# A hybrid attention and state-space step on one core: TensorE's order in the loop over head groups, fixed as written

## The chip, the cores and the metric

The kernel runs on one core of a Trainium2 chip. The metric is the device time of one execution in microseconds (us), median of several runs. Engines: TensorE (PE, with PEld for its weight loads), VectorE (DVE), ScalarE (ACT), GpSimd (POOL), and SyncE (SP), which issues the DMAs.

## The reference, cut to what matters

Two layers run over 128 context tokens and 512 latent tokens. Layer 0 is attention. Layer 1, where the change lies, is a Mamba-2 scan in both directions over chunks of 128 tokens:

```python
proj = h @ w_in
z, xbc, dt = split(proj)
xbc = silu(depthwise_conv_centred(xbc, conv_w, conv_b))       # -> xs, bs, cs
# per chunk, per direction
y_diag = einsum('bclsgr,bcsgrp->bclgrp', cb[..., None] * decay, x)
states = einsum('bclgn,bclgrp->bcgrpn', b, x * decay_end[..., None])
h_next = h * chunk_decay + states
y_off  = einsum('bclgn,bcgrpn->bclgrp', c, h_prev) * exp(a_cs)
# both directions and the skip term summed
y = rms_norm(y * silu(z), gnorm_w)
out = y @ w_out
```

There are 32 heads in 4 groups of 8. A group shares B and C.

## The kernel before, in words

Tokens lie in five tiles t of 128: tile 0 is the context, tiles 1 to 4 the latent tokens. `layer1` loops over the head groups g (0 to 3), and in each over ten steps j. A step emits, in this order: `off` (L1172: the state's part of the output), `advance` (L1179: the next state), `prompt_state` (L1150), `decay` (a small product C times B, L1116, and the chain that makes the decay matrix), `diag` (L1134: the diagonal products of one tile, then L1137: four transposes of Y), loads, and then the step's fill work: a projection of 128 columns (`proj_T`, L914, 48 products, "a unit" below) for the next group's x, B and C or for this group's z, and transposes of the unit before (`x_turn`, `b_turn`, L1007). In group 3 the fills of steps 3 to 8 are pieces of the output projection (`part_mm`, L1366, 24 products each), fed by `part_turn`, which loads gated rows back from DRAM into the two buffers named `u`.

One decay matrix passes through a chain: two DMAs into buffers `am0` and `am1` (`a_load`, L1112), two selects on POOL (L1120, L1121), sixteen exponentials on ACT (L1125), an add on POOL (L1126), a product on DVE (L1127), then `diag`. There are two `am0` buffers and one `am1`. So the load of `am0` for tile 1 (fourth in the order 0, 2, 3, 1, 4) waits for the diagonal products of tile 2, and that of `am1` for tile 4 waits for tile 1's add.

TensorE's small outputs go to a PSUM pool `a` of four buffers, and units to a pool `pj` of two. `gate` multiplies by z, squares and sums (L1086, L1078, L1090); `gate_last` does it in group 3, and `final_rstd` (L1371) takes the sum over partitions with a product on TensorE.

What is emitted is not the order on the engines: the kernel is built with a scheduler that plays the program against its own cost model and writes out an order for each engine and for SP's queue. Each engine then runs its own list strictly in that order.

Of the kernel before, what the change touches and what calls it, by code (L numbers as in the profile page):

```python
# [26 lines left out]
NG = 4  # L27
# [26 lines left out]
class Hybrid:  # L54
# [955 lines left out]
    def layer1(self, hT, wp, pj, pa, ctx):  # L1010
        nc, tc, A, O = self.nc, self.tc, self.A, self.O
# [19 lines left out]
        def x_turn(g, jj):  # L1031
            xt = xts[g]
            self.turn(wcur["u"], pa, lambda t, ps: nc.scalar.copy(xt[:, t, P * jj:P * jj + P], ps))

        def bc_unit(g, which):
            if which == 0:
                wcur["bc"] = self.load_w(wp, A["l1_w_in"], [(2 * DI + P * g, P), (2 * DI + P * (NG + g), P)])
                bcs[g] = {"T": self.tl(sp, [P, NT, P], tag="T")}
            wcur["u"] = bcs[g][which] = self.conv_chunk(16 + 4 * which + g, wcur["bc"], P * which, hT, pj, self.tl(sp, [P, TW - 3], tag=f"B{which}"))

        def b_turn(g):
            T = bcs[g]["T"]
            self.turn(bcs[g][0], pa, lambda t, ps: nc.scalar.copy(T[:, t, :], ps))
# [16 lines left out]
        def z_unit(g, jj):  # L1060
            zs, off_ = z_tile(g, jj)
            ps = self.proj_T(pj, wcur["z"], off_, P, hT)
            z_evac(zs, ps[:, 0:TW - 2])
# [41 lines left out]
        def y_init(g, t):  # L1105
            y = Y[:, t].rearrange("p j q -> p (j q)")
            nc.gpsimd.tensor_tensor(h3(y), h3(xts[g][:, t, :]), bch(self.dsk[:, 8 * g:8 * g + 8]), op=ALU.mult)

        def a_load(g, t):
            af = W[g, t] = [self.tl(wk, [P, 8, P], tag=f"am{d}", bufs=2 - d) for d in range(2)]  # L1110
            for d in range(2):
                nc.sync.dma_start(out=af[d].rearrange("p h l -> p (h l)"), in_=self.acd[t][g][d].rearrange("h l -> (h l)").unsqueeze(0).to_broadcast([P, 8 * P]))  # L1112
# [16 lines left out]
        def diag(g, t):  # L1129
            w = W.pop((g, t))[0]  # L1130
            pd = self.tl(pa, [P, 4, P], tag="a")
            for h in range(8):
                e = 64 * (h % 2)
                nc.tensor.matmul(pd[e:e + 64, h // 2, :], xts[g][:, t, HD * h:HD * h + HD], w[:, h, :], start=True, stop=True)  # L1134
            pr = self.tl(pa, [P, 4, P], tag="a")
            for i in range(4):
                nc.tensor.transpose(pr[:, i, :], Y[:, t, i, :], self.ident)  # L1137
            nc.scalar.copy(Y[:, t], pd)
            nc.vector.tensor_tensor(Y[:, t], Y[:, t], pr, op=ALU.add)
# [5 lines left out]
        def prompt_state(g, d):  # L1145
            xw = Xw.pop((g, 0, d))
            T = bcs[g]["T"]
            ps = self.tl(pa, [P, 4, P], tag="a")
            for j in range(4):
                nc.tensor.matmul(ps[:, j, :], xw[:, P * j:P * j + P], T[:, 0, :], start=True, stop=True)  # L1150
            st = self.tl(wk, [P, 4, P], tag="ym")
            nc.scalar.copy(st, ps)
            dst = O["new_state_f" if d == 0 else "new_state_b"][0, 8 * g:8 * g + 8].rearrange("h p n -> (h p) n").rearrange("(j q) n -> q j n", q=P)
            nc.sync.dma_start(out=dst, in_=st)
# [6 lines left out]
        def state_init(g, d):  # L1161
            st = St.pop((g, d))
            ps = self.tl(pa, [P, 4, P], tag="a")
            for j in range(4):
                nc.tensor.transpose(ps[:, j, :], st[:, j, :], self.ident)
            H[d] = self.tl(wk, [P, 512], tag=f"h{d}", bufs=2)
            nc.scalar.copy(H[d], ps.rearrange("p j q -> p (j q)"))

        def off(g, t, d):
            y = Y[:, t].rearrange("p j q -> p (j q)")  # L1170
            ps = self.tl(pa, [P, 512], tag="a")
            nc.tensor.matmul(ps, bcs[g][1][:, ts(t)], H[d], start=True, stop=True)  # L1172
            m = self.tl(wk, [P, 512], tag="ym")
            nc.vector.tensor_tensor(h3(m), h3(ps), bch(self.ea[:, t, sl(g, d)]), op=ALU.mult)  # L1174
            nc.gpsimd.tensor_tensor(y, y, m, op=ALU.add)  # L1175

        def advance(g, t, d):
            p2 = self.tl(pa, [P, 512], tag="a")
            nc.tensor.matmul(p2, bcs[g]["T"][:, t, :], Xw.pop((g, t, d)), start=True, stop=True)  # L1179
            old, h = H[d], self.tl(wk, [P, 512], tag=f"h{d}", bufs=2)  # L1180
            H[d] = h
            nc.vector.tensor_tensor(h3(h), h3(old), bch(self.cd[:, t, sl(g, d)]), op=ALU.mult)
            nc.vector.tensor_tensor(h, p2, h, op=ALU.add)

        def lag(f, g, j, before=None):
            u = wcur.get("u")
            f(g, j)
            v = wcur["u"]
            if before:
                wcur["u"] = u  # L1190
                before[0](*before[1:])
                wcur["u"] = v
# [4 lines left out]
        def part_turn(t, g):  # L1197
            if t not in early:
                early[t] = self.tl(self.h1, [P, 2, 12, P], F32R, tag=f"h1{t - 2}")
            self.yT[t, g] = [early[t][:, i, 4 * g:4 * g + 4] for i in range(2)]  # L1200
            self.y_turn(t, g, wk, "u")

        def part_mm(k0):
            self.weng = [nc.vector]
            w = self.load_wide(wp, A["l1_w_out"], k0)
            for t in (2, 3):
                if k0 == 0:
                    ps = self.tl(pj, [P, 1024], tag="pj")
                    self.PS[t] = [ps[:, 0:512], ps[:, 512:1024]]
                self.out_mm(t, w, k0)  # L1210
# [14 lines left out]
        for d in range(2):  # L1225
            state_load(0, d)
        seq = [0, 2, 3, 1, 4]
        for g in range(NG):
            last = g == NG - 1
            nx = lambda jj: (lambda: lag(x_unit, g + 1, jj, (x_turn, g + 1, jj - 1) if jj else None))  # L1230
            zf = lambda jj: (lambda: z_unit(g, jj))
            if last:
                pt_ = lambda t, k: (lambda: part_turn(t, k))
                pm_ = lambda k: (lambda: part_mm(k))
                fl = {0: [zf(0), zf(1)], 1: [zf(2)], 2: [zf(3), pt_(2, 0), pt_(3, 0)], 3: [pt_(2, 1), pt_(3, 1), pm_(0)],
                      4: [pt_(2, 2), pt_(3, 2), pm_(2)], 5: [pm_(4)], 6: [pm_(6)], 7: [pm_(8)], 8: [pm_(10)]}
            else:
                fl = {j: [nx(j)] for j in range(4)}
                fl.update({4: ([zf(0)] if g else []) + [lambda: x_turn(g + 1, 3)], 5: [zf(1)] if g else [], 6: [lambda: bc_unit(g + 1, 0)], 7: [lambda: bc_unit(g + 1, 1)], 8: [zf(2), lambda: b_turn(g + 1)], 9: [zf(3)]})
            for j in range(10):  # L1240
                if 1 <= j <= 4:
                    for d in range(2):
                        off(g, j if d == 0 else 5 - j, d)
                if 1 <= j <= 3:
                    for d in range(2):
                        advance(g, j if d == 0 else 5 - j, d)
                if j in (4, 5):
                    prompt_state(g, j - 4)
                if j == 0:
                    a_load(g, seq[0])  # L1250
                    for d in range(2):
                        state_init(g, d)
                    for t in (0, 1, 4, 2, 3):
                        y_init(g, t)
                if j < 5:
                    decay(g, seq[j])
                for t in {1: (0,), 3: (2, 3), 4: (1,), 5: (4,)}.get(j, ()):
                    diag(g, t)
                if j < 4:
                    a_load(g, seq[j + 1])  # L1260
                if j <= 2:
                    for d in range(2):
                        weighted(g, j + 1 if d == 0 else 4 - j, d)
                if j == 3:
                    for d in range(2):
                        weighted(g, 0, d)
                for f in fl.get(j, []):
                    f()
                if last:
                    for t in {4: (2, 3), 5: (1, 0), 6: (4,)}.get(j, ()):  # L1270
                        gate_last(t)
                        self.final_rstd(t, pa)
                    continue
                if j == 6:
                    gate(g, 0)
                    for d in range(2):
                        state_load(g + 1, d)
                if j == 9:
                    gate(g, 1)

        def hold(t, q, tags, pool):
            self.yT[t, q] = [self.tl(pool, [P, 4, P], F32R, tag=i, bufs=1 if tags[0] != tags[1] else 2) for i in tags]
# [180 lines left out]
```

## Time and profile before

| | us |
|---|---|
| median of 3 runs (1002.45 to 1007.39) | 1005.37 |
| the profiled execution's own time | 1004.88 |
| its span, first to last instruction | 1003.10 |
| TensorE busy in the span | 935.6 (93%) |
| loop over head groups, about | 515 to 910 |

The profile is of one execution; TensorE's granted clock has a mean of 0.984 of full speed in it. Positions such as 588.16 are us from the span's start.

### The profile page before, as it was taken

The page shows a single profiled execution, that of the slowest core. Times are in us where ns is not written, and L with a number is a line of the kernel's source. Part 1 is how long each engine was busy: PE and PEld are TensorE (multiplying, and loading weights), DVE is VectorE, ACT ScalarE, POOL GpSimd, SP SyncE. Part 2 cuts the span into 40 slices and gives each one's busy share as a digit, 9 for nine tenths or more (in the row PEclk, how much of TensorE's full clock was granted, in tenths as well). Part 3 has the DMA queues.
Part 4 walks back from the last instruction along what each step waited for, and adds up shares of the span by engine and source line. Part 5 has one row for each costly group of instructions (what it writes and reads, how often), then busy time and mean ns, then how long its engine had stood idle before and what let it go on. Part 6 is the DMA issues. An engine that isn't in the chain of part 4 may idle for free.

```text
span 1003.1 us, 17041 instructions
## 1 busy us (share of the span) xinstructions
PE 935.6 (93%) x6466; PEld 832.5 (83%) x6466; DVE 667.6 (67%) x1034; ACT 515.1 (51%) x1212; POOL 500.0 (50%) x447
## 2 busy tenths in 40 slices
PE   5988999999999989989899998998999899879997
PEld 3887879879997789979898897898978898658786
DVE  4478665766675765874758657866666756887663
ACT  5346666757775753332545565465426552463340
POOL 3354235226370352463278778968497767653000
PEclk9999999999999999999999999999999999999999
DMA  9943243211113233343244354244424433445752
GB/s 312 354 126 97 93 119 125 84 54 43 43 54 95 88 103 106 106 123 84 69 132 144 106 172 133 85 156 142 133 85 156 144 119 96 137 140 201 263 190 88
DMA packets 90354, 127.91 MB, mean 128 GB/s; under 512 B 6816, under 2 KB 65312, under 8 KB 90272
## 3 DMA queue, kind: packets, MB, share of 16 engines
q1 hardware_dynamic: 90272, 126.82, 39.5%
q8 instruction: 51, 0.84, 0.4%
q14 instruction: 31, 0.25, 0.1%
HBM read 115.10 MB, written 11.70 MB: 126 GB/s over the span
## 4 chain that ended last, share of the span: by engine, by line
PE 54%; DVE 14%; POOL 11%; issue 8%; DMA 7%; ACT 6%; SPq 0%; POOLq 0%; DVEq 0%; ACTq 0%
PE pj L914 14%; PE pp L283 8%; PE po L668 3%; PE a L841 3%; PE pj L1366 3%; PE acc L379 3%; PE S L630 3%; PE pt L658 3%; DMA am<-acd 2%; PE pp L175 2%; POOL ys L1175 2%; POOL am L1126 2%; POOL xw L1143 2%; DVE ys L1086 2%; ACT am L1125 2%
## 5 line engine op out<-in xcount | busy, mean ns | idle before, releaser
L914 PE MATMUL pj<-h,wh 128*128 128x322 f32 (+1 forms) x1248 | 299.4, 326 | 7.3 <-DVE B L999 3.8
L914 PEld LDWEIGHTS pj<-h,wh 128*128 128x128 f32 (+1 forms) x1248 | 212.3, 190 | 19.4 <-issue 12.6
L74 POOL TENSOR_TENSOR wl<-raw,wh 128x512 fp32r<-128x512 f32 (+1 forms) x70 | 131.8, 1893 | 185.1 <-ACT wh L73 183.4
L914 PE MATMUL pj<-h,wl 128*128 128x322 f32 (+1 forms) x624 | 198.0, 318 | 0.0
L73 ACT CAST wh<-raw 128x1024 fp32r<-128x1024 f32 (+1 forms) x117 | 103.2, 912 | 79.7 <-DMA raw<-in_l_w_out 27.9
L1125 ACT ACTIVATE am<-am,nb 128x128 f32<-128x128 f32 x320 | 98.7, 390 | 86.1 <-POOL am L1121 67.0
L914 PEld LDWEIGHTS pj<-h,wl 128*128 128x128 f32 (+1 forms) x624 | 118.7, 190 | 2.5 <-issue 2.1
L283 PE MATMUL pp<-wh,big 128*128 128x256 f32 x576 | 113.3, 286 | 0.5 <-ACT sg L527 0.5
L283 PEld LDWEIGHTS pp<-wh,big 128*128 128x128 f32 x576 | 92.3, 190 | 0.8 <-ACT sg L527 0.7
L283 PE MATMUL pp<-wl,big 128*128 128x256 f32 x288 | 81.7, 284 | 0.0
L74 DVE TENSOR_TENSOR wl<-raw,wh 128x1024 fp32r<-128x1024 f32 x47 | 61.6, 1317 | 23.7 <-ACT wh L73 23.6
L74 DVE TENSOR_TENSOR pl<-pt,ph 128x512 fp32r<-128x512 f32 (+1 forms) x100 | 59.2, 600 | 25.8 <-ACT ph L73 25.2
L633 DVE TENSOR_REDUCE nm<-S 128x1 f32<-128x640 f32 x64 | 52.4, 820 | 14.0 <-PE S L630 13.1
L73 ACT CAST ph<-pt 128x512 fp32r<-128x512 f32 (+1 forms) x100 | 51.4, 518 | 18.9 <-PE pt L658 14.1
L1126 POOL TENSOR_TENSOR am<-am,am 128x1024 f32<-128x1024 f32 x20 | 51.1, 2553 | 15.6 <-ACT am L1125 15.5
L637 ACT ACTIVATE Pt<-S,nm 128x640 f32<-128x640 f32 x64 | 51.3, 803 | 12.5 <-PE pt L658 9.5
L283 PEld LDWEIGHTS pp<-wl,big 128*128 128x128 f32 x288 | 54.9, 190 | 0.0
L1366 PE MATMUL pj<-wh,h 128*128 128x512 f32 x160 | 52.5, 402 | 1.0 <-ACT h L73 1.0
L658 PE MATMUL pt<-cst,Pt 128*128 128x128 f32 x320 | 50.8, 276 | 2.7 <-DVE pl L74 2.3
L1175 POOL TENSOR_TENSOR ys<-ys,ym 128x512 f32<-128x512 f32 x32 | 49.2, 1549 | 7.0 <-DVE ym L1174 6.9
L630 PE MATMUL S<-kT,qT 128*128 128x320 f32 x256 | 51.3, 326 | 1.5 <-ACT Pt L637 1.5
L841 PE MATMUL a<-wh,big 128*128 128x256 f32 x256 | 46.8, 283 | 0.0
(348 smaller groups left out, 2169.9 us busy)
## 6 DMA issues: line engine op xcount, KB each, us to landing
raw<-in_l_w_in SPq DMA_DIRECT2D x48, 512.0 KB
am<-acd SPq DMA_DIRECT2D x40, 512.0 KB
raw<-in_l_w_out SPq DMA_DIRECT2D x36, 512.0 KB
og<-in_l_mod_w SPq DMA_DIRECT2D x29, 512.0 KB
raw<-in_l_w_in SPq DMA_DIRECT2D x25, 256.0 KB
mw<-in_l_mod_w SPq DMA_DIRECT2D x11, 512.0 KB
raw<-in_l_mod_w SPq DMA_DIRECT2D x8, 512.0 KB
yzd<-ys SPq DMA_DIRECT2D x6, 640.0 KB
```

The lines of the kernel that those rows point to most:

```text
L73: (heng.tensor_copy if heng else self.nc.scalar.copy)(hi, src)
L74: (eng or self.nc.vector).tensor_tensor(lo, src, r32(hi), op=ALU.subtract)
L283: nc.tensor.matmul(ps, a[:, k, cs], b[:, k, :], start=k == 0 and a is hi and b is w[0], stop=k == KD - 1 and a is lo)
L630: nc.tensor.matmul(S[:, 192 + 320 * q:512 + 320 * q], qTs[g, t][:, h, :], kT[:, hl, 320 * q:320 * q + 320], start=hl == 0, stop=hl == 1)
L633: nc.vector.tensor_reduce(c["m"], c["s"], axis=AX.X, op=ALU.max, negate=True)
L658: nc.tensor.transpose(pt[:, 2 * i + j, :], Pts[j][:, kt * P:kt * P + P], self.ident)
L841: self.nc.tensor.matmul(ps, self.ohl[a][:, k, ts], w[b][:, k, :], start=k == 0 and i == 0, stop=k == KD - 1 and i == 2)
L914: nc.tensor.matmul(ps[0:m, 190 + 322 * half:512 + 322 * half], w[b][:, k, off:off + m], hT[s][:, k, 322 * half:322 * half + 322], start=fi ...
L1125: nc.scalar.activation(af[d][:, h, :], af[d][:, h, :], AF.Exp, bias=self.nb[:, t, i:i + 1], scale=1.0)
L1126: nc.gpsimd.tensor_tensor(af[0], af[0], af[1], op=ALU.add)
L1175: nc.gpsimd.tensor_tensor(y, y, m, op=ALU.add)
L1366: nc.tensor.matmul(self.PS[t][n], y[a][:, kk, :], b, start=k0 + k == 0 and i == 0, stop=k0 + k == 15 and i == 2)
```

## The change

The whole loop over g is put under a manual schedule for TensorE: there its instructions stand as emitted. The other engines and SP's queue are still ordered by the scheduler. Two things are moved in the emission: `diag` goes behind the step's fills, and group 3's `final_rstd` of a tile goes two steps later than its `gate_last`.

```diff
-        for g in range(NG):
+        with tc.manual_schedule(engines={mybir.EngineType.PE}):
+            for g in range(NG):
...
                 if j < 5:
                     decay(g, seq[j])
-                for t in {1: (0,), 3: (2, 3), 4: (1,), 5: (4,)}.get(j, ()):
-                    diag(g, t)
...
                 for f in fl.get(j, []):
                     f()
+                    for t in {1: (0,), 3: (2, 3), 4: (1,), 5: (4,)}.get(j, ()):
+                        diag(g, t)
                 if last:
-                    for t in {4: (2, 3), 5: (1, 0), 6: (4,)}.get(j, ()):
-                        gate_last(t)
-                        self.final_rstd(t, pa)
+                        for t in {6: (2, 3), 7: (1, 0), 8: (4,)}.get(j, ()):
+                            self.final_rstd(t, pa)
+                        for t in {4: (2, 3), 5: (1, 0), 6: (4,)}.get(j, ()):
+                            gate_last(t)
```

TensorE at the start of group 0, before the change: `a_6735` and `a_6742` are the initial states' transposes, `a_6754` the first C times B, `pj_6802` the first unit of the loop (its rows alternate between three operands; 46 of the 48 stand ahead of L1116).

```order
L1165 MATMUL a_6735<-cst_60,st_1396_6727 128x128 x4
L1165 MATMUL a_6742<-cst_60,st_1397_6729 128x128 x4
L914 MATMUL pj_6802<-h_1183_5264,wh_6792 128x322
L914 MATMUL pj_6802<-h_1184_5265,wh_6792 128x322
...
L1116 MATMUL a_6754<-B_1392_6663,B_1388_6599 128x128
L914 MATMUL pj_6802<-h_1184_5265,wh_6792 128x322
L914 MATMUL pj_6802<-h_1183_5264,wl_6791 128x322
```

The same place in the change:

```order
L1165 MATMUL a_6737<-cst_60,st_1396_6727 128x128 x4
L1165 MATMUL a_6744<-cst_60,st_1397_6729 128x128 x4
L1116 MATMUL a_6756<-B_1392_6663,B_1388_6599 128x128
L914 MATMUL pj_6804<-h_1183_5264,wh_6794 128x322
L914 MATMUL pj_6804<-h_1184_5265,wh_6794 128x322
```

The small product has gone ahead of the whole unit.

TensorE at the end of group 0's scan, before: the diagonal products of tile 1 (`a_7320`) and tile 4 (`a_7353`); between the first row and the last 72 products of units stand where the dots are.

```order
L1116 MATMUL a_7292<-B_1392_6663,B_1388_6599 128x128
...
L1134 MATMUL a_7320<-am_1447_7040,xt_6209 64x128 x8
L1137 MATMUL a_7329<-cst_60,ys_6019 128x128 x4
L1007 MATMUL a_7336<-cst_60,u_7210 128x128 x4
L1007 MATMUL a_7342<-cst_60,u_7210 128x128
...
L1150 MATMUL a_7345<-T_6598,xw_1476_7208 128x128 x4
...
L1134 MATMUL a_7353<-am_1473_7202,xt_6209 64x128 x8
L1137 MATMUL a_7362<-cst_60,ys_6019 128x128 x4
```

In the change, from the two transposes that follow the same C times B (tile 1 is `a_7331`, tile 4 `a_7355`, `pj_7383` the first unit behind them):

```order
L1007 MATMUL a_7322<-cst_60,u_7180 128x128 x4
L1007 MATMUL a_7328<-cst_60,u_7180 128x128
L1134 MATMUL a_7331<-am_1447_7042,xt_6209 64x128 x8
L1137 MATMUL a_7340<-cst_60,ys_6019 128x128 x4
L1150 MATMUL a_7347<-T_6598,xw_1472_7178 128x128 x4
L1134 MATMUL a_7355<-am_1469_7172,xt_6209 64x128 x8
L1137 MATMUL a_7364<-cst_60,ys_6019 128x128 x4
L914 MATMUL pj_7383<-h_1183_5264,wh_7372 128x322
```

No unit stands between these any more; group 0 has none in steps 4 and 5.

ACT in group 3, before: the evictions of the diagonal products of tiles 2 and 3 (L1138) among the casts of rows that come back from DRAM (`h_...<-u_...`) and of weights (`wh_...`).

```order
L73 CAST h_1851_10127<-u_10128 128x512
L73 CAST xw_1944_10630<-grow_1056_4660 128x512
L1138 COPY ys_6019<-a_10187 128x512
L1138 COPY ys_6019<-a_10203 128x512
L73 CAST h_1851_10127<-u_10227 128x512
L1125 ACTIVATE am_1846_10068<-am_1846_10068,nb_6375 128x128 x8
L73 CAST h_1853_10133<-u_10232 128x512
L73 CAST h_1851_10127<-u_10335 128x512
```

And in the change:

```order
L73 CAST h_1851_10129<-u_10197 128x512
L73 CAST h_1853_10135<-u_10202 128x512
L73 CAST h_1851_10129<-u_10321 128x512
L73 CAST h_1853_10135<-u_10326 128x512
L73 CAST wh_10402<-raw_10403 128x1024
L73 CAST wh_10402<-raw_10407 128x1024
L1138 COPY ys_6019<-a_10243 128x512
L1138 COPY ys_6019<-a_10259 128x512
```

The two evictions now stand behind four casts of reloaded rows and two of weights.

## Rows read from the trace of the kernel before

**Rows 1.** The page: busy time, share of the span and instructions of each engine.

```profile
PE 935.6 (93%) x6466; PEld 832.5 (83%) x6466; DVE 667.6 (67%) x1034; ACT 515.1 (51%) x1212; POOL 500.0 (50%) x447
```

**Rows 2.** Stretches: length, TensorE busy (instructions), granted clock, DMA share, GB/s.

```profile
515.00:604.00 89.00, 86.08 (x575) 0.98 0.43 131
604.00:705.00 101.00, 93.16 (x619) 0.98 0.40 124
705.00:809.00 104.00, 99.08 (x673) 1.00 0.40 125
809.00:899.00 90.00, 80.72 (x472) 0.97 0.40 126
```

**Rows 3.** TensorE's waits, 500 to 930: total us, times, longest.

```profile
PE a L1371 <- POOL ssq L1098: 4.3, 1, 4.3
PE a L1116 <- DVE h L1183: 4.0, 1, 4.0
...
PE pj L914 <- DVE u L999: 1.8, 1, 1.8
PE a L1134 <- issue: 1.7, 1, 1.7
PE a L1116 <- DVE ym L1174: 1.3, 1, 1.3
...
PE a L1137 <- POOL ys L1175: 1.0, 1, 1.0
```

**Rows 4.** TensorE in order of time, group 0's start: start, us, instruction.

```profile
514.78 1.04 PE L1165 MATMUL a<-cst,st 128*128 128x128 f32 x8
```

**Rows 5.** VectorE in order of time, the same place.

```profile
519.03 0.83 DVE L999 SCALAR_TENSOR_TENSOR B<-pj,B 128x641 f32<-128x641 f32 x1
```

**Rows 6.** TensorE in order of time, group 0, tile 2 and later.

```profile
561.17 1.09 PE L1134 MATMUL a<-am,xt 128*64 128x128 f32 x16
562.20 0.66 PE L1137 MATMUL a<-cst,ys 128*128 128x128 f32 x4
...
572.50 1.05 PE L1150 MATMUL a<-T,xw 128*128 128x128 f32 x8
```

**Rows 7.** GpSimd in order of time there; brackets: idle before, what ended it.

```profile
566.21 1.09 POOL L1120 TENSOR_SCALAR_AFFINE_SELECT am<-am 128x1024 f32<-128x1024 f32 x1 [3.92 <-DMA am<-acd]
...
579.86 1.09 POOL L1121 TENSOR_SCALAR_AFFINE_SELECT am<-am 128x1024 f32<-128x1024 f32 x1 [2.90 <-DMA am<-acd]
583.59 2.39 POOL L1126 TENSOR_TENSOR am<-am,am 128x1024 f32<-128x1024 f32 x1 [2.63 <-ACT am L1125]
585.93 4.04 POOL L1143 TENSOR_TENSOR xw<-xt,ws 128x512 f32<-128x512 f32 x3
```

**Rows 8.** VectorE in order of time, tile 4's decay product.

```profile
586.01 2.05 DVE L1127 TENSOR_TENSOR am<-am,cb 128x1024 f32<-128x1024 f32 x1 [0.52 <-POOL am L1126]
```

**Rows 9.** Stretches for the clock: length, TensorE busy, granted clock, DMA share, GB/s.

```profile
548.69:552.09 3.40, 3.40 (x15) 0.50 0.56 154
560.00:580.00 20.00, 20.00 (x160) 1.00 0.49 146
...
623.79:627.19 3.40, 2.88 (x12) 0.50 0.17 61
```

**Rows 10.** The chain in order of time: one whole unit, start and us.

```profile
507.25 7.16 PE pj L914 x48
```

**Rows 11.** The page's costliest groups: busy, mean ns, idle before.

```profile
L73 ACT CAST wh<-raw 128x1024 fp32r<-128x1024 f32 (+1 forms) x117 | 103.2, 912 | 79.7 <-DMA raw<-in_l_w_out 27.9
```

**Rows 12.** TensorE in order of time, group 3.

```profile
854.28 1.88 PE L1172 MATMUL a<-h,B 128*128 128x512 f32 x4
...
863.09 0.79 PE L1366 MATMUL pj<-wh,h 128*128 128x512 f32 x1 [0.96 <-ACT h L73]
```

**Rows 13.** SyncE in order of time, group 3.

```profile
860.79 0.32 SPq L1352 DMA_DIRECT2D u<-yzd  x1
```

**Rows 14.** VectorE in order of time, group 3.

```profile
865.07 0.68 DVE L1355 TENSOR_TENSOR u<-u,cols 128x512 f32<-128x512 f32 x1
```

More of the change, by code (lines that the diff above doesn't have):

```diff
@@ L1227, in layer1 @@
         seq = [0, 2, 3, 1, 4]
-        for g in range(NG):
[L1229 to L1256, printed above, removed]
-                for t in {1: (0,), 3: (2, 3), 4: (1,), 5: (4,)}.get(j, ()):
-                    diag(g, t)
[L1259 to L1268, printed above, removed]
-                if last:
-                    for t in {4: (2, 3), 5: (1, 0), 6: (4,)}.get(j, ()):
-                        gate_last(t)
-                        self.final_rstd(t, pa)
[L1273 to L1279, printed above, removed]
@@ new lines, in layer1 @@
+        with tc.manual_schedule(engines={mybir.EngineType.PE}):
+            for g in range(NG):
+                last = g == NG - 1
+                nx = lambda jj: (lambda: lag(x_unit, g + 1, jj, (x_turn, g + 1, jj - 1) if jj else None))
+                zf = lambda jj: (lambda: z_unit(g, jj))
+                if last:
+                    pt_ = lambda t, k: (lambda: part_turn(t, k))
+                    pm_ = lambda k: (lambda: part_mm(k))
+                    fl = {0: [zf(0), zf(1)], 1: [zf(2)], 2: [zf(3), pt_(2, 0), pt_(3, 0)], 3: [pt_(2, 1), pt_(3, 1), pm_(0)],
+                          4: [pt_(2, 2), pt_(3, 2), pm_(2)], 5: [pm_(4)], 6: [pm_(6)], 7: [pm_(8)], 8: [pm_(10)]}
+                else:
+                    fl = {j: [nx(j)] for j in range(4)}
+                    fl.update({4: ([zf(0)] if g else []) + [lambda: x_turn(g + 1, 3)], 5: [zf(1)] if g else [], 6: [lambda: bc_unit(g + 1, 0)], 7: [lambda: bc_unit(g + 1, 1)], 8: [zf(2), lambda: b_turn(g + 1)], 9: [zf(3)]})
+                for j in range(10):
+                    if 1 <= j <= 4:
+                        for d in range(2):
+                            off(g, j if d == 0 else 5 - j, d)
+                    if 1 <= j <= 3:
+                        for d in range(2):
+                            advance(g, j if d == 0 else 5 - j, d)
+                    if j in (4, 5):
+                        prompt_state(g, j - 4)
+                    if j == 0:
+                        a_load(g, seq[0])
+                        for d in range(2):
+                            state_init(g, d)
+                        for t in (0, 1, 4, 2, 3):
+                            y_init(g, t)
+                    if j < 5:
+                        decay(g, seq[j])
+                    if j < 4:
+                        a_load(g, seq[j + 1])
+                    if j <= 2:
+                        for d in range(2):
+                            weighted(g, j + 1 if d == 0 else 4 - j, d)
+                    if j == 3:
+                        for d in range(2):
+                            weighted(g, 0, d)
+                    for f in fl.get(j, []):
+                        f()
+                    for t in {1: (0,), 3: (2, 3), 4: (1,), 5: (4,)}.get(j, ()):
+                        diag(g, t)
+                    if last:
+                        for t in {6: (2, 3), 7: (1, 0), 8: (4,)}.get(j, ()):
+                            self.final_rstd(t, pa)
+                        for t in {4: (2, 3), 5: (1, 0), 6: (4,)}.get(j, ()):
+                            gate_last(t)
+                        continue
+                    if j == 6:
+                        gate(g, 0)
+                        for d in range(2):
+                            state_load(g + 1, d)
+                    if j == 9:
+                        gate(g, 1)
```

## The prediction, made before the change was run

> **What bounds the kernel now.** I read the page's first part, then TensorE's busy time by stretches that follow the head groups, then its waits in the loop, then four places in order of time. TensorE is busy for 93% of the span [rows 1]. In the four stretches of the loop it is idle for 2.92, 7.84, 4.92 and 9.28 us [rows 2], 24.96 us in all. So the loop runs at TensorE's pace, with chains on the other engines close behind it, and no order of its work can give back more than about 25 us and what the clock loses after idle time. Group 3's idle time holds one wait of 4.3 us for the sum of squares (L1371, L1098); group 1 starts with one of 4.0 us for the state's update (L1116, L1183) [rows 3]. The reader should see that 25 us stand spread over some sixteen waits, because whenever one chain was late the scheduler had put products of a unit there.
>
> **What the change moves.** It adds and removes no work. It makes every place where a small product waits hold back all that is emitted behind it, the units too. So I take each place where a product now stands ahead of a unit that used to cover it.
>
> **Group 0's start.** The first C times B used to stand behind 46 products of a unit; now it directly follows the state's transposes. It needs the convolved C. The transposes end at 514.78 + 1.04 = 515.82 [rows 4], C's last operation on VectorE at 519.03 + 0.83 = 519.86 [rows 5]. TensorE waits **+4.0**. Groups 1 to 3 have two z units between C's projection and this place, and don't. In step 1 the next C times B needs the PSUM buffer of `off`, whose eviction now stands on VectorE behind the decay product of tile 0 and a weight split; I take **+1.5**, between 0 (it comes first after all) and 3 (a decay product of 2.05 [rows 8] and one operation more).
>
> **The end of group 0's scan.** This is the largest term. From tile 2's diagonal products (end D) two decay chains follow each other through `am0` and `am1`. The first: its load is there 3.95 us after the products that free its buffer (561.17 + 1.09 = 562.26 to 566.21 [rows 6, 7]), the select takes 1.09, the exponentials 2.63 (the add's wait for them), the add 2.39, the decay product 2.05 [rows 7, 8]. With nothing in the way that is 12.1 after D. In POOL's new order the add has an `off` addition, tile 4's select and another `off` addition ahead of it after the first select: about 1 us more, so 13.1. The second chain starts at the first's add, at 11.1: load, select, exponentials, add and product, 12.1 again, and 2 more because the add stands behind a select of the next group, whose load waits for tile 1's diagonal products. Tile 4's products can start at 25.3.
>
> TensorE has little for this time. Behind D stand one set of transposes (0.66), tile 3's products and transposes (1.75), two `off`, one `prompt_state` (1.05), C times B and five transposes: about 6 us with their evictions. It waits from 6.3 to 13.1, does tile 1 and `prompt_state` (2.8), and waits from 15.9 to 25.3: 6.8 + 9.4 = **+16.2**. Before, 72 products of units lay here, 1.5 units of 7.16 us [rows 10], and the wait was under 1 us. Lower bound 13, with nothing in the way on POOL; upper 20, if the loads take a microsecond or two longer each.
>
> **What goes with it.** The other engines catch up in these waits. Group 0's old waits (2.92 [rows 2], among them 1.8 for a convolution [rows 3]) and those at group 1's start (7.84 less 2.9 at its end: 4.9 [rows 2]), which came from gating that VectorE had not done yet, should go: **-7.8**. Between 0 and that.
>
> **Groups 1 and 2.** Here z units stand in steps 4 and 5, 7.16 us each. Tile 1: 6 + 7.2 = 13.2 of cover for 13.1, no wait. Tile 4: between the two stand 2.8 + 7.2 = 10.0 less the first microsecond of overlap, for a chain of 12.2: about 2.7 in each group, 5.4. Group 2's three waits of 1.7, 1.3 and 1.0 [rows 3] are of this same kind and are replaced: **+1.4**, between -4 and +8.
>
> **Group 3.** The wait of 4.3 for the sum of squares goes, two steps give it time. Against it: the first output products need rows reloaded and split into a buffer that the last z unit frees. That unit ended at about 854.28, the first output product ran at 863.09, 8.8 later [rows 12]; `off`, `advance` and C times B fill half of this, tile 2's diagonal products used to stand in the rest and now stand behind: 4.4. Then ACT: the evictions of tiles 2 and 3 now follow four casts of reloaded rows. A reload takes 4.3 us from issue (860.79 [rows 13]) to use (865.07 [rows 14]), and there are two `u` buffers, so the four come in two rounds of some 6.3 us with multiply, cast and split; then two weight casts of 0.91 [rows 11]. That lets ACT go 23.5 us after the z unit, while TensorE needs the first eviction after 17: 6.5. Tile 1 and 4 then wait for their chains behind 24 output products each: about 4 and 4. Sum 18.9 against the 9.3 of before [rows 2]: **+9.6**, between -4.3 (only the old wait goes) and +16.
>
> **The clock.** After idle stretches of 1.8 and 4.0 us (to 548.6 and 624.3) the granted clock is 0.50, the lower of its two levels, for 3.4 us [rows 9], which costs about half of them, 1.7. Group 0, group 1 and twice group 3 have such a stretch now. I count six after: **+3.4**, between 0 and 7.
>
> **Sum.** 4.0 + 1.5 + 16.2 - 7.8 + 1.4 + 9.6 + 3.4 = 28.3 on the profiled execution's 1004.88 (its span 1003.10 and 1.78 around it), which lies 0.5 below the median: **1033**.
>
> **A rule against this reading.** In 560 to 580 units and small products alternate, and the granted clock is 1.00 with TensorE busy throughout [rows 9]; what went before each fall was idle time, not alternation. The Trainium skill, Perfetto Trace Analysis, section Matmul Optimizations, says that the engine scales with its use, so that matmuls should run back to back in batches. By that, 48 unbroken products would be the better order, and the rival of a faster kernel below would hold; this trace agrees with the rule on idle time only.
>
> **Rivals.**
> *Only group 0 loses.* Group 3's evictions don't hold TensorE up, and groups 1 and 2 stay as they were: 4.0 + 1.5 + 16.2 - 7.8 + 1.7 = 15.6, so 1020. For it: the waits of group 3 rest on a long chain of mine; against it: ACT's rows stand in that order whatever the times. Chance 0.24.
> *Small products in a row wait for PSUM.* With four `a` buffers and nine or ten small outputs between units, each of some twelve such rows waits a microsecond for an eviction: 1033 + 12 = 1045. For it: before, four waits of 1 to 4 us in rows 3 were of that sort with units between; against it: evictions of 0.7 fit into the products' time when ACT and VectorE are free. Chance 0.14.
> *No change.* Chains on POOL and ACT run faster than in rows 7 (13 at the end of group 0), group 3 gains its 4.3 and the clock costs nothing more: 4.0 + 13 - 7.8 - 4.3 = 4.9, less some of groups 1 and 2: 1007. Chance 0.07.
> *Faster.* All other waits of the loop go, since units run unbroken and other engines always have one unit's time to catch up; with them three of the four half-clock stretches. That is -25.0 - 5.1 + 4.0 + 16.2 = -9.9: 995. It decides as long as all new waits together stay below 25.0 + 5.1 = 30 us less the 5 that can be told; group 0's alone would, but tile 4's chain is longer than its cover in every group. Chance 0.05.
>
> **How the numbers follow.** The forecast's own case (1026 to 1041) has 0.50. The range of 8 in 10 runs from the lower end of the group 0 case, 1012, to inside the PSUM case, 1047; outside lie the no-change and the faster case (0.12) and half of the PSUM case (0.07). About 0.5%, 5 us, is what a measurement of this kernel can tell from no change. Faster by more: 0.05; within: 0.07; slower: 0.88.
>
> **What would show it.** In the trace of after: a wait of 4 us before L1116 near 516; two of about 7 and 9 us before L1134 in group 0, released by the decay product L1127, with POOL's add L1126 behind it, and no product of a unit between tile 1 and tile 4; waits of 2 to 3 us before tile 4's products in groups 1 and 2; in group 3 an `off` (L1172) that waits for ACT's eviction; more stretches at half clock; no wait before the sum of squares. I am wrong if group 0 shows less than 10 us before its diagonal products, or if group 3 is idle for less than the 9.3 us of before.

## The result and the profile after

The changed kernel takes 1034.99 us (median of 4 runs, 1032.85 to 1038.52) against 1006.27 for the kernel before on the same chip: 1.0303 times, 95% interval 1.0271 to 1.0334. The profiled execution is 1033.24 us with a span of 1031.4, 28.3 above the span of before. The prediction was 1033, slower.

The page's first part, for [rows 1]:

```profile
PE 944.1 (92%) x6466; PEld 842.2 (82%) x6466; DVE 651.4 (63%) x1034; ACT 516.4 (50%) x1212; POOL 482.6 (47%) x447
```

The number of instructions is the same. TensorE is busy for 8.5 us more, which is the same work at a lower clock, and idle for 19.8 more.

The stretches by head group, cut at the transposes of the initial states (L1165), the last one to the span's end; columns as in [rows 2]. After:

```profile
513.30:630.10 116.80, 92.47 (x574) 0.88 0.33 106
630.10:738.80 108.70, 101.51 (x668) 0.97 0.37 119
738.80:841.80 103.00, 99.14 (x670) 1.00 0.41 131
841.80:1031.40 189.60, 171.34 (x853) 0.97 0.47 155
```

Before, cut in the same way:

```profile
514.80:603.80 89.00, 86.08 (x575) 0.98 0.43 131
603.80:704.90 101.10, 93.26 (x620) 0.98 0.40 125
704.90:808.50 103.60, 98.69 (x669) 1.00 0.40 125
808.50:1003.10 194.60, 178.55 (x902) 0.98 0.48 159
```

Idle is length less busy. It goes from 2.92 to 24.33 us in group 0, from 7.84 to 7.19 in group 1, from 4.91 to 3.86 in group 2, and from 16.05 to 18.26 behind that: +21.4, -0.65, -1.05 and +2.2, in sum 21.9. Busy time over the four goes from 456.57 to 464.46, +7.9, and the loop starts 1.5 us earlier: 21.9 + 7.9 - 1.5 = 28.3. (One unit of 48 products that stood in the last stretch stands in group 1's now, so lengths of single rows are not to be compared, idle times are.) Nearly all of the loss is in group 0, and there the granted clock is 0.88.

TensorE's waits in the loop, for [rows 3] (total us, times, longest):

```profile
PE a L1134 <- DVE am L1127: 21.2, 3, 9.3
PE pj L1368 <- DVE h L74: 5.1, 1, 5.1
PE a L1116 <- DVE ym L1174: 4.7, 2, 4.0
PE a L1116 <- DVE B L999: 4.1, 1, 4.1
PE a L1134 <- ACT wh L73: 3.2, 2, 1.7
PE pj L914 <- DVE B L999: 2.9, 1, 2.9
PE a L1134 <- ACT am L73: 1.7, 1, 1.7
...
PE a L1172 <- ACT ys L1138: 1.0, 1, 1.0
```

The first row is the diagonal products' wait for the decay product. Two of its three are in group 0, 9.25 us before tile 1 and 7.31 before tile 4:

```profile
580.81 1.98 PE L1134 MATMUL a<-am,xt 128*64 128x128 f32 x16 [9.25 <-DVE am L1127]
592.20 1.98 PE L1134 MATMUL a<-am,xt 128*64 128x128 f32 x16 [7.31 <-DVE am L1127]
```

The wait for the sums of squares is gone, and so is the one of 4.0 us for the state's update.

GpSimd in order of time at that place (start, us, instruction, idle time before and what ended it), for the chain of [rows 7]:

```profile
574.05 1.09 POOL L1120 TENSOR_SCALAR_AFFINE_SELECT am<-am 128x1024 f32<-128x1024 f32 x1 [1.98 <-DMA am<-acd]
575.11 1.26 POOL L1175 TENSOR_TENSOR ys<-ys,ym 128x512 f32<-128x512 f32 x1
576.33 2.34 POOL L1126 TENSOR_TENSOR am<-am,am 128x1024 f32<-128x1024 f32 x1
...
586.28 1.09 POOL L1120 TENSOR_SCALAR_AFFINE_SELECT am<-am 128x1024 f32<-128x1024 f32 x1 [2.57 <-DMA am<-acd]
587.34 1.04 POOL L1143 TENSOR_TENSOR xw<-xt,ws 128x512 f32<-128x512 f32 x1
588.34 2.35 POOL L1126 TENSOR_TENSOR am<-am,am 128x1024 f32<-128x1024 f32 x1
```

Each add L1126 that TensorE waits for stands behind a select whose load is not there yet: 1.98 us before the first, 2.57 before the second. The exponentials that the two adds read ended on ScalarE at 573.31 and 586.19, so the adds started 3.0 and 2.2 us later than their own data allowed, because of what stands ahead of them on GpSimd.

The place at group 0's start, on TensorE:

```profile
518.45 0.49 PE L1116 MATMUL a<-B,B 128*128 128x128 f32 x2 [4.08 <-DVE B L999]
```

The product that used to stand behind 46 others of a unit now waits 4.08 us for the convolution of C.

Stretches of the same trace for the clock (columns as in [rows 9]): two behind the second long wait, and one around the end of group 1's wait of 3.99 us before C times B.

```profile
592.20:597.00 4.80, 4.80 (x28) 0.50 0.54 198
598.00:600.00 2.00, 2.00 (x16) 1.00 0.00 0
669.40:676.20 6.80, 5.41 (x20) 0.50 0.07 22
```

A mean between 0.50 and 1.00 is a mixture of the two levels, 1.2 and 2.4 GHz. The low level reaches into stretches where TensorE is busy again without a gap (592.2 to 597.0: busy for all of 4.80 us at 0.50; from 598 on it is 1.00). That is the part of the loss that the table of waits does not show.

### The profile page after: what moved, and what is told of

The parts are those of the page before. It is cut to its first block, busy times and chain, and to the rows that moved or that the text cites. A ratio compares the mean times of both kernels' runs of the same rounds, so it can differ in the third digit from the quotient of the medians.

```text
span 1031.4 us, 17045 instructions
## 1 busy us (share of the span) xinstructions
PE 944.1 (92%) x6466; PEld 842.2 (82%) x6466; DVE 651.4 (63%) x1034; ACT 516.4 (50%) x1212; POOL 482.6 (47%) x447
## 4 chain that ended last, share of the span: by engine, by line
PE 64%; DVE 14%; DMA 7%; POOL 6%; issue 5%; ACT 4%; SPq 0%; POOLq 0%; DVEq 0%; ACTq 0%
PE pj L914 22%; PE pp L283 9%; PE pj L1368 4%; PE po L668 3%; PE acc L379 3%; PE a L841 3%; PE S L630 3%; PE pt L658 3%; DMA am<-acd 2%; PE pp L175 2%; DMA raw<-in_l_w_out 2%; DVE wl L74 1%; PE a L1172 1%; ACT wh L73 1%; PE a L1179 1%
## 5 line engine op out<-in xcount | busy, mean ns | idle before, releaser
L914 PE MATMUL pj<-h,wh 128*128 128x322 f32 (+1 forms) x1248 | 289.2, 320 | 4.1 <-DVE B L999 2.9
L74 POOL TENSOR_TENSOR wl<-raw,wh 128x512 fp32r<-128x512 f32 (+1 forms) x70 | 131.0, 1881 | 207.2 <-ACT wh L73 205.5
L74 DVE TENSOR_TENSOR wl<-raw,wh 128x1024 fp32r<-128x1024 f32 x47 | 64.2, 1378 | 29.0 <-ACT wh L73 28.9
L74 DVE TENSOR_TENSOR pl<-pt,ph 128x512 fp32r<-128x512 f32 (+1 forms) x100 | 59.2, 600 | 25.8 <-ACT ph L73 25.1
L1127 DVE TENSOR_TENSOR am<-am,cb 128x1024 f32<-128x1024 f32 x20 | 32.7, 1634 | 56.2 <-POOL am L1126 55.9
L1126 POOL TENSOR_TENSOR am<-am,am 128x1024 f32<-128x1024 f32 x20 | 48.3, 2414 | 6.8 <-ACT am L1125 6.8
L1175 POOL TENSOR_TENSOR ys<-ys,ym 128x512 f32<-128x512 f32 x32 | 45.2, 1417 | 10.6 <-DVE ym L1174 10.5
```

The source lines that it names most:

```text
L74: (eng or self.nc.vector).tensor_tensor(lo, src, r32(hi), op=ALU.subtract)
L914: nc.tensor.matmul(ps[0:m, 190 + 322 * half:512 + 322 * half], w[b][:, k, off:off + m], hT[s][:, k, 322 * half:322 * half + 322], start=fi ...
L1126: nc.gpsimd.tensor_tensor(af[0], af[0], af[1], op=ALU.add)
```

## The experiments

Each ratio is to the kernel before, timed on the same chip, with its 95% interval; a per cent is about 10 us. The theory: an order fixed on TensorE makes each late small product hold back the projections emitted behind it; the largest place is the end of group 0's scan, which has no projection in steps 4 and 5. Rivals: the two moves cost, not the order; or the loss is spread over all groups.

**The fixed order without the moves.**

```diff
+                    for t in {1: (0,), 3: (2, 3), 4: (1,), 5: (4,)}.get(j, ()):
+                        diag(g, t)
                     if j < 4:
                         a_load(g, seq[j + 1])
...
                     for f in fl.get(j, []):
                         f()
-                    for t in {1: (0,), 3: (2, 3), 4: (1,), 5: (4,)}.get(j, ()):
-                        diag(g, t)
...
-                        for t in {6: (2, 3), 7: (1, 0), 8: (4,)}.get(j, ()):
-                            self.final_rstd(t, pa)
                         for t in {4: (2, 3), 5: (1, 0), 6: (4,)}.get(j, ()):
                             gate_last(t)
+                            self.final_rstd(t, pa)
```

> TensorE's order as emitted, with the diagonal products ahead of the step's projection and the sums of squares at their old step, so that only one of the three parts of the change is made. My theory: the fixed order is what costs, and the two moves soften it. Without the moves each diagonal product stands 7.2 us (one projection) closer to the decay that it waits for, and the sums of squares stand right behind the gate whose result they read: some 4 us of wait for two of the three sums and 2 to 5 us for each diagonal tile of groups 1 to 3 come on top: 1045 to 1065 us, slower than the changed kernel. Rival (the moves are what costs, the order is harmless): 1000 to 1012 us. Rival (the moves do nothing): 1032 to 1037 us.

Measured: 1045.51 us, ratio 1.0408 (1.0366 to 1.045). In total as expected, at the low end of the range and 10 us above the changed kernel. But not place by place; its stretches, cut as above:

```profile
512.90:616.40 103.50, 90.53 (x574) 0.93 0.37 119
616.40:731.30 114.90, 101.56 (x669) 0.99 0.36 113
731.30:845.10 113.80, 104.81 (x668) 0.94 0.39 119
845.10:1044.20 199.10, 173.57 (x854) 0.95 0.44 148
```

The order binds the whole loop in both kernels, and the counts agree within two records, so these lengths can be set beside those of the changed kernel. Groups 1, 2 and what follows are 6.2, 10.8 and 9.5 us longer without the moves. In the last of them TensorE now waits for the sums of squares, while other waits there are shorter:

```profile
PE a L1372 <- POOL ssq L1098: 11.2, 2, 8.2
```

Group 0 is 13.3 us shorter. My expectation that the moves soften the order everywhere is wrong there: with tiles 2 and 3 of the diagonal ahead of step 3's projection, that projection stands behind the release of the decay buffers and covers the chain of tile 1 (it runs from 564.5 to 572.5, and tile 1's products start at 576.19 without a wait). With those tiles moved behind it, nothing does. The hole in group 0 is thus made by the order and the move together.

**Projections put into the hole.**

```diff
+                if g == 0:
+                    fl[4].append(fl[6].pop())
+                    fl[5].append(fl[7].pop())
                 for j in range(10):
```

> The changed kernel, with group 0's two B and C projections of the next group emitted in steps 4 and 5 instead of 6 and 7, so that TensorE has 7.2 us of work ahead of each of the two diagonal tiles that waited 9.25 and 7.31 us. My theory: these two waits are the largest term of the loss; they fall to about 2 us and below, and the low clock behind them goes too: 1034 minus 12 to 18, 1016 to 1022 us. Rival (the waits only move to steps 6 and 7, which have lost their units, or the end of the group is bound by the chain of VectorE and GpSimd and not by TensorE's order): 1028 to 1036 us.

Measured: 1014.45 us, ratio 1.0098 (1.007 to 1.0127), 20 us below the changed kernel, somewhat more than expected. TensorE from 570 to 600:

```profile
570.00:600.00 30.00, 28.46 (x212) 1.00 0.49 161
```

In the changed kernel the same 30 us were

```profile
570.00:600.00 30.00, 13.44 (x86) 0.66 0.36 127
```

The wait before tile 1 is 1.46 us now, the one before tile 4 is gone, and the clock does not fall. The same chains run on the other engines. Group 0 is 23.9 us shorter than in the changed kernel (92.90 against 116.80), and some 5 us of it come back in groups 1 and 3. So 20 us of the loss hung on what stood on TensorE's queue there, and not on those chains being slower.

**The first C times B behind a projection.**

```diff
-                    if j < 5:
+                    if j < 5 and g + j:
                         decay(g, seq[j])
...
                     for f in fl.get(j, []):
                         f()
+                    if g + j == 0:
+                        decay(g, seq[j])
```

> The same, and group 0's first C by B product emitted behind the first projection of the group instead of ahead of it. My theory: its wait of 4.08 us, and the low clock that followed it (a projection took 8.9 us in place of 7.4), go: 4 to 6 us below the run before, 1011 to 1017 us. Rival (the decay comes 7.4 us later, and the diagonal product of tile 0 in step 1 then waits as much): within 1.5 us of the run before.

Measured: 1016.37 us, ratio 1.0117 (1.0088 to 1.0146). The rival holds: no gain over the run before. The wait of 4.08 us is gone, and the step behind it has three, 5.5 us in sum, where the run before had one of 0.3 (TensorE's waits of this kernel from 500 to 555):

```profile
PE a L1179 <- DVE ym L1174: 2.3, 1, 2.3
PE a L1172 <- ACT xt L1033: 1.7, 1, 1.7
PE a L1007 <- DVE u L999: 1.5, 1, 1.5
```

The rival had named the diagonal product of tile 0 as what waits; it is the transposes, `off` and `advance`. The wait bought VectorE and ScalarE the time that they needed here, and without it they were late one projection further on.

**The last group's diagonal products ahead of the first output product.**

```diff
+                    if last and j == 3:
+                        pm_0 = fl[3].pop()
                     for f in fl.get(j, []):
                         f()
...
                         diag(g, t)
+                    if last and j == 3:
+                        pm_0()
```

> The same, and in step 3 of the last group the diagonal products of tiles 2 and 3 emitted ahead of the first output product, which waited 5.13 us for the split of a weight on VectorE. My theory: the two tiles are 2 to 3 us of work that covers as much of the wait, and half clock followed that wait: 2 to 4 us below the run before, 1008 to 1014 us. Rival (the diagonal products' own evictions stand ahead of the split on VectorE and push it as far back): within 1.5 us of the run before.

Measured: 1009.62 us, ratio 1.0053 (1.0033 to 1.0073), 6.8 us below the run before. That is more than the 2 to 4 expected, but by the ratios it is 6.4 with some 3 us either way. The wait of 5.1 us is gone; it was for the split of reloaded rows (`h`, L74), not of a weight as I had written. TensorE's longest waits from 850 to 960 are

```profile
PE a L1134 <- DVE am L1127: 3.2, 1, 3.2
PE a L1137 <- POOL ys L1175: 2.7, 1, 2.7
```

against 5.1 and 4.9 us in the run before. I had counted only the covered wait; the one before the later diagonal product shrank too, and the one of 2.7 is new. From the start of group 3 to the span's end, the run before and this run:

```profile
825.70:1015.90 190.20, 171.96 (x854) 0.97 0.45 154
821.30:1007.10 185.80, 172.26 (x854) 0.97 0.47 158
```

The stretch that the edit touches is 4.4 us shorter, with 4.7 us less idle time. As much again lies ahead of it in this pair of traces, 2.8 us of that ahead of the loop, and is not shown to come from the edit.

**The two gaining edits without the decay's move.** The edit of the second and of the fourth experiment together.

> The changed kernel with the two edits that gained, the B and C projections of group 0 in steps 4 and 5 and the last group's diagonal products ahead of the first output product, and without the move of the first decay, which lost 1.9 us. My theory: 1014.5 minus the 6.8 us that the last group's edit gave: 1006 to 1010 us, 0 to 0.6% above the kernel before. Rival (the last group's edit gained because of what the decay's move did to VectorE): 1010 to 1015 us.

Measured: 1010.38 us, ratio 1.0041 (1.0023 to 1.0059). The time lies just above the range expected and in the rival's, but the kernel before took 1006.49 us beside this run and 1003.66 beside those that the ranges were worked out from. By ratios the sum expected was 1.0098 - 0.0064 = 1.0034; it lies in the interval, and the rival's 1010 to 1015 us, 1.0063 to 1.0113, does not. With TensorE's order fixed, no version tried was faster than the kernel before.

**The order free in group 0 alone.**

```diff
-        with tc.manual_schedule(engines={mybir.EngineType.PE}):
-            for g in range(NG):
+        for g in range(NG):
+            with (tc.manual_schedule(engines={mybir.EngineType.PE}) if g else ExitStack()):
```

> The changed kernel, with the emitted order binding TensorE in groups 1 to 3 alone; in group 0 the scheduler orders it again as before. My theory: group 0 carries 16.6 us of wait at the end of its scan, 4.1 at its start, some 3 of wait at its last turn and 3 to 4 of low clock behind them, of which the old order had about half of the last two: 1034 minus 20 to 25, 1010 to 1016 us, and the remaining 5 to 9 us above the kernel before lie in group 3. Rival (the loss is spread over the four groups, and group 0 has a quarter to a third of it): 1024 to 1028 us.

Measured: 1009.48 us, ratio 1.0034 (1.0016 to 1.0053), a little below the low end expected. Its stretches, cut so that the counts agree within seven with those of the changed kernel:

```profile
514.10:602.90 88.80, 84.75 (x573) 1.00 0.41 130
602.90:714.40 111.50, 102.10 (x675) 0.97 0.40 125
714.40:818.90 104.50, 98.51 (x663) 1.00 0.39 127
818.90:1008.90 190.00, 172.18 (x854) 0.96 0.46 155
```

Group 0 is 28.0 us shorter than in the changed kernel; group 1 gives back 2.8 and the rest 1.9. So group 0 holds nearly all of the difference to the kernel before, by the ratios 27 of 30 us.

**The order free in group 3 alone.** The same edit with `if g < NG - 1`.

> The changed kernel, with the emitted order binding TensorE in groups 0 to 2 alone. By the prediction group 3 had 9.6 us of the loss, which would leave 1025 us. By the trace of the changed kernel its waits there are 12.6 us, those of both moves without the order 7.0, so the order costs 5.6 us there and 1 to 3 of low clock: 1026 to 1030 us. Rival (TensorE's end in group 3 hangs on the weights' loads alone): 1033 to 1036 us.

Measured: 1032.02 us, ratio 1.0261 (1.0238 to 1.0284), some 4 us below the changed kernel by the ratios (0 to 8 by their intervals), 3 by the medians, and in neither range. The 9.6 us of the prediction are refuted. My reading of the trace (6.6 to 8.6 us) was 2 to 6 us too high for the whole kernel, but near for the stretch from group 3 to the span's end, which is now

```profile
847.10:1030.70 183.60, 171.89 (x854) 0.98 0.47 160
```

This is 6.0 us shorter than in the changed kernel, with 6.5 us less idle time. In this trace the loop starts 2.0 us later, and its first three groups, whose order did not change, take 3.3 us more. The long `am` waits of group 0 are all there (9.24 and 7.53 us).

**The two moves without the fixed order.** TensorE's order stays the scheduler's.

```diff
-                for t in {1: (0,), 3: (2, 3), 4: (1,), 5: (4,)}.get(j, ()):
-                    diag(g, t)
...
                 for f in fl.get(j, []):
                     f()
+                for t in {1: (0,), 3: (2, 3), 4: (1,), 5: (4,)}.get(j, ()):
+                    diag(g, t)
                 if last:
+                    for t in {6: (2, 3), 7: (1, 0), 8: (4,)}.get(j, ()):
+                        self.final_rstd(t, pa)
                     for t in {4: (2, 3), 5: (1, 0), 6: (4,)}.get(j, ()):
                         gate_last(t)
-                        self.final_rstd(t, pa)
```

> The kernel before, with the scheduler's order of TensorE, and both moves: diagonal products emitted behind the step's projection, sums of squares two steps later. My theory: the moves themselves cost nothing, since a scheduler that is free on TensorE takes the diagonal products when their data are due: 1000 to 1008 us, so that all of the 29 us comes with the fixed order. Rival (the moves push the diagonal products' evictions back on ScalarE and VectorE and cost on their own): 1012 to 1030 us.

Measured: 996.73 us, ratio 0.9912 (0.9887 to 0.9937): the moves do not cost, they gain about 9 us, which neither theory had said. The fixed order then costs 38 us against the same program without it (1034.99 less 996.73).

**Each move alone, without the fixed order.** First the sums of squares, then the diagonal products.

> The kernel before, with TensorE's order left to the scheduler as there, and only the last sums of squares emitted two steps later, behind more output products. My theory: the wait of 4.3 us for the sums of squares goes, with little else changed: 1 to 5 us below the kernel before, 1000 to 1004 us. Rival (the scheduler already placed them as well as their data allow, and TensorE waits for the scan's end anyway): within 1 us of it, 1003 to 1006 us.

Measured: 1005.39 us, ratio 0.9999 (0.998 to 1.0018). The rival holds, though the wait itself shrank from 4.3 us [rows 3] to

```profile
PE a L1372 <- POOL ssq L1098: 2.0, 2, 1.4
```

Another wait (1.8 us before a diagonal product) came up close by.

> The kernel before, with TensorE's order left to the scheduler, and only the diagonal products emitted behind the step's projection. Both moves without the fixed order ran at 996.7 us, 9.8 below the kernel before, and the move of the sums alone at the time of before. My theory: the diagonal products' move is what gained, since ScalarE, VectorE and GpSimd then take what the next projection and the scan need ahead of the diagonal's copies: 996 to 1000 us. Rival (the gain needs both, since the sums' wait of 4.3 us only goes when the scan ends earlier): 1001 to 1005 us.

Measured: 998.26 us, ratio 0.9922 (0.9899 to 0.9945): the diagonal products' move is the one that gains. Its stretches, cut at L1165 as above:

```profile
512.80:601.50 88.70, 84.68 (x573) 1.00 0.41 130
601.50:698.10 96.60, 92.78 (x621) 0.98 0.41 131
698.10:811.50 113.40, 107.57 (x717) 0.98 0.40 128
811.50:996.50 185.00, 172.02 (x854) 0.98 0.47 159
```

Idle time in the four is 4.02, 3.82, 5.83 and 12.98 us, against 2.92, 7.84, 4.91 and 16.05 before: the gain is in group 1 (4.0) and from group 3 on (3.1), and groups 0 and 2 lose 2.0. The span is 6.6 us shorter; the loop also starts 2 us earlier, which the move is not shown to cause. The wait for the sums of squares is not among this kernel's waits at all, though they stand where they stood. Which operation of the other engines makes the room was not tested.

**The last group's edit without the fixed order.** The diff of the fourth experiment, on both moves without the order.

> Both moves without the fixed order, and the last group's diagonal products of step 3 ahead of the first output product. Under the fixed order this gave 4 to 7 us. Theory: a scheduler that is free on TensorE already fills that place, so within 2 us of both moves alone: 995 to 999 us. Rival (the emitted place decides on VectorE and ScalarE too, and the gain comes again): 990 to 994 us.

Measured: 998.44 us, ratio 0.9922 (0.9899 to 0.9945), like both moves alone. Where the order is fixed this edit gave some 6 us (6.4 and 5.7 by the ratios of its two pairs); where it is free, nothing that these runs can tell.

**The B and C projections two steps earlier, without the fixed order.**

```diff
-                fl.update({4: ([zf(0)] if g else []) + [lambda: x_turn(g + 1, 3)], 5: [zf(1)] if g else [], 6: [lambda: bc_unit(g + 1, 0)], 7: [lambda: bc_unit(g + 1, 1)], 8: [zf(2), lambda: b_turn(g + 1)], 9: [zf(3)]})
+                fl.update({4: [lambda: x_turn(g + 1, 3), lambda: bc_unit(g + 1, 0)], 5: [lambda: bc_unit(g + 1, 1)] + ([zf(0)] if g else []), 6: [zf(1)] if g else [], 8: [zf(2), lambda: b_turn(g + 1)], 9: [zf(3)]})
```

> Both moves without the fixed order, and the B and C projections of the next group emitted in steps 4 and 5 in all groups, the first two z projections a step later. With both moves TensorE still waited 6.9 us (4.1 at most) for VectorE's convolution of C or B ahead of a group's last projection. Theory: VectorE has those convolutions done before the gates come, and 3 to 6 us go: 991 to 994 us. Rival (the gates come later and VectorE's backlog moves to the next group's start): 996 to 1002 us.

Measured: 990.57 us, ratio 0.9851 (0.9828 to 0.9873), just below the range expected: the fastest version, 15 us below the kernel before. With both moves alone, TensorE waited for VectorE's convolution of B or C

```profile
PE pj L914 <- DVE B L999: 6.9, 3, 4.1
```

and with the earlier projections

```profile
PE pj L914 <- DVE B L999: 2.2, 1, 2.2
```

That is not the whole gain. Over the loop and what follows TensorE is idle for 2.0 us less than with both moves alone (21.93 against 23.91), since other waits grew (the transposes' for the convolution, L1007, from 0.3 to 1.9). It is busy for 3.0 us less with the same products (452.97 against 455.99), at a mean granted clock of 0.990 against 0.982. The loop starts 1.1 us earlier.

## Why the prediction was right

The time (1033 against 1034.99, span +28.3 against +28.3) and the mechanism were right. (The median of before plus 28.3 is 1033.7; the prediction named the 0.5 between the two and left it out.) That the sum agrees to the tenth is luck: its terms are off by up to 7.4 us, in both directions. Neither of its signs of being wrong showed: the waits before group 0's diagonal products are 16.6 us, not under 10, and those of group 3 are 12.5 us, not under 9.3.

- **Group 0's start**, +4.0: measured 4.08, released by the convolution as foreseen. The +1.5 for C times B in step 1 was not there; 0, the lower bound. The third experiment adds what the prediction did not see: this wait is no loss by itself, since VectorE and ScalarE are late behind it if it goes.
- **The end of group 0's scan**, +16.2: measured 9.25 + 7.31 = 16.56. The two parts were put at 6.8 and 9.4. The first add L1126 stood behind tile 4's select and that select's load, 3.0 us in place of the 1 us allowed for. The second wait was shorter because TensorE's work between the two took 4.1 us at the low clock and not 2.8, and the chain 11.4 and not 12.2 (its decay product 1.22 and not 2.05). No product of a unit stands between, and the releaser is L1127, with L1126 behind it, as written. Filling the hole brought 20 us: the 16.6, less 1.5 that remained, and the low clock.
- **Old waits that go**, -7.8: too large. The wait for the state's update at group 1's start went, but group 0's last unit waits 2.9 us for a convolution, and C times B in group 1 waits 4.0 for an eviction of `off` (L1174). With the next term, groups 1 and 2 are 1.7 less idle than before; the prediction's two terms gave 4.9 - 1.4 = 3.5 for them.
- **Groups 1 and 2**: waits of 2.7 before tile 4's products were foreseen; 1.73 and 1.48 were measured. (The table puts them down to a cast on ScalarE, but in group 1 the decay product ended at 708.01 and the products started at 708.11.)
- **Group 3**, +9.6: the worst term, +2.2 idle against the kernel before. (With its order freed the stretch is 6.0 us shorter, but then the moves gain there too.) The wait for the output product was 5.1 (4.4 foreseen) and the sums' wait went. Mis-sized was ScalarE's delay: `off` waited 1.0 us instead of 6.5 for the first eviction. ScalarE came to it 20.5 us after the last z unit's end (880.6 to 901.1), not 23.5, and TensorE to `off` after 20.1 us, not 17, since its own wait and the low clock behind it had held it up:

```profile
880.28 0.32 PE L914 MATMUL pj<-h,wl 128*128 128x322 f32 x1
898.72 0.62 ACT L73 CAST h<-u 128x512 fp32r<-128x512 f32 x1 [3.36 <-DVE u L1357]
899.25 1.99 ACT L73 CAST wh<-raw 128x1024 fp32r<-128x1024 f32 x2
901.14 1.06 ACT L1138 COPY ys<-a 128x512 f32<-128x512 f32 x2
901.77 1.98 PE L1172 MATMUL a<-h,B 128*128 128x512 f32 x4 [1.04 <-ACT ys L1138]
```

  The order on ScalarE was right (casts of rows, two of weights, then the eviction); the two rounds of reloads had been put 3 us too long. Tiles 1 and 4 waited 4.7 and 1.7 us, 4 and 4 foreseen.
- **The clock**, +3.4: too small, 7.9 us more busy time for the same products. I had counted six stretches at low clock, 1.7 us each, against four before. There were four before, but there are seven now. By an estimate from busy time and granted clock in steps of half a microsecond, four of them cost some 1.7 us each, and those behind the waits that end at 592.2, 670.8 and 890.0 cost 2.3 to 2.8. Of group 3's error of 7.4 us it makes up for 4.5; group 0's idle time (21.4, its terms gave 18.8) and the old waits of groups 1 and 2 (1.8) more than do the rest, and the loop's start was 1.5 us earlier.

Of the rivals, the one with group 0 alone was nearest in place (free order there leaves 1.0034), but not in size: it counted 15.6 us, group 0's part is 25 to 28. It came short because it let all the old waits go and gave the clock 1.7 us. The rows of small products waiting for PSUM exist, but are few: 4.7 us before C times B (L1116, released by L1174) in place of 12, and old waits of the same kind went. No change fell with group 0's hole, which is at its full price. The faster kernel fell because the other waits did not go: groups 1 and 2 are only 1.7 us less idle, and what follows is 2.2 more. Group 0's hole stood in that rival's own sum and would not have refuted it alone. The Trainium skill, Perfetto Trace Analysis, section Matmul Optimizations, asks for matmuls back to back in batches. This case agrees with that only as far as no batch has a late product at its head: the units run unbroken in the changed kernel, and it is the slower one.

What the prediction did not ask is whether the moves gain by themselves. It took order and moves as one. Order alone costs 41 us by its ratio, the moves alone save 9, both together cost 30; that these nearly add up is chance, since the moves cost 13 us in group 0 and save 26 in the other places once the order is fixed.

## What to carry to other kernels

Before fixing one engine's order, look in the emitted program for stretches with no large work between a product and the chain that it waits for; each such stretch costs what the chain lasts beyond the work that stands there, and one of them here cost 20 of 29 us. A place written later in the program can gain while the scheduler stays free, so try the moves without the fixed order first. And a wait that is removed may have been the time in which another engine caught up: look at what comes one projection later.

## What the runs showed of the hardware

The granted clock fell after a single wait of 1.8 us in the kernel before [rows 3, 9]. In the changed kernel it was 0.50 through 4.80 us of unbroken products behind the second long wait (592.2 to 597.0), and 1.00 from 598 on. In sum the low clock cost 7.9 us more busy time than before. Where the hole was filled, the granted clock over the same 30 us was 1.00.
